# All weight sums in the second FFN, and seven block products in the third

## The chip, the cores and the metric

The kernel runs on one core of one Trainium2 chip. The time is device microseconds of one execution; the kernel before took 922.86 us, the median of three runs (922.39 to 922.95). One execution was profiled.

## The reference, cut to what matters

A trunk of two layers on x of shape (1, 256, 1024), all float32: each layer is half an FFN, a mixer, half an FFN.

```python
h = h + 0.5 * swiglu(rms_norm(h, ffn1_norm[layer]), ffn1_w_gate[layer], ffn1_w_up[layer], ffn1_w_down[layer])
h = h + ab_mixer(...) if layer % 2 == 0 else h + c_mixer(...)
h = h + 0.5 * swiglu(rms_norm(h, ffn2_norm[layer]), ffn2_w_gate[layer], ffn2_w_up[layer], ffn2_w_down[layer])
# swiglu(x, g, u, d) = (silu(x @ g) * (x @ u)) @ d, with D_FF = 2816
```

A last RMS norm follows. So there are four FFNs; the text calls them first (phase 0), second (phase 2), third (phase 3) and last (phase 5). Phases 1 and 4 are the mixers. The second FFN and the third stand next to each other.

## The kernel before, in words

Every product of activations and weights is made of three matmuls (`mm3`, L388 to L390): both operands are split into a high part (`whi`, `xTh`, `hTh`) and the rest (`wlo`, `xTl`, `hTl`), and high x high, rest x high and high x rest are added in one PSUM bank. There are eight banks.

`Stream` brings the weights in one order for the whole kernel, by chunks of up to 128 x 2048. SP issues the loads into three `raw` buffers (L201); ScalarE copies the high part (L249) and VectorE subtracts it (L256), into one of four pairs of buffers (`SPL`). When a chunk has been used up, `free` gives its buffers back, and the next split and the next load are written down there.

An FFN first makes 22 gate and up products (steps n = 0 to 21, one chunk of 48 matmuls each), turns each pair into two tiles of the hidden matrix (`gated`), and then multiplies by the down weights. In the plain form the four blocks of 256 output columns are made one after the other, each from three chunks of 8, 8 and 6 tiles; `pair` (L437, L438, L424, L427) adds a finished block to x and forms `xTh` and `xTl` for the next stage. Behind the second or third gate/up product of a stage `everywhere` makes the norm: VectorE and ScalarE split the sum of squares into `acch` and `accl` (L393), TensorE multiplies both by ones (L481, L482), and a row comes out by which `gated` scales.

In the first FFN alone (`WOVEN = (0,)`) half of the down projection, 512 of 1024 output columns, has another form: a pair of hidden tiles and two tiles of 256 columns make a 2 x 2 product of blocks, which needs seven block products instead of eight. The sums of weight blocks are formed in the `raw` buffer behind the load (L263 to L267), those of hidden blocks in `gated` (L738 to L740). The products (`seven_products`) go to four banks of their own and are woven between the gate/up chunks from the fifth pair on (`LAG = 4`), and between the down chunks. They come out with tokens on the partitions, so `gather_first` adds them up and `turned` transposes them back (eight transposes, L787).

The last FFN uses seven products for nine of its eleven pairs, and needs sums of its weight blocks. These are made earlier: `begin_sums` loads a chunk into `blocks` (L666), three or four subtractions on VectorE form the sums in place (L670 to L676), and `keep` stores them to device memory (L682). `AHEAD` names the steps where a load is issued; the subtractions are written one step later, the stores two. Loads and stores stand in SP's queue behind the weight load last issued before them.

Inside each engine the order is fixed when the program is built: a planner goes through the instructions by their place in the program, with durations that it assumes, and takes the first that it believes to be ready. On the chip each engine then follows that order. `issue_after` binds an instruction behind another on its engine. Each stage opens a pool for its own tiles (`fp` for an FFN, `mp` for a mixer) and closes it at its end; the next stage's pool takes the same memory.

Of the kernel before, what the change touches and what calls it, by code (L numbers as in the profile page):

```python
# [11 lines left out]
F32R = mybir.dt.float32r  # L12
# [8 lines left out]
FT = FF // 128  # L21
# [15 lines left out]
LINE, SHIFT = 64, 16  # L37
EDGE, GAP = 56, 240

RESET, RESHIFT = 3, 52  # L40
# [5 lines left out]
SPARE = 2  # L46
AHEAD = [(phase, n) for phase in (2, 3) for n in (4, 8, 12, 16)] + [(3, 19)]

WOVEN = (0,)
LAG = 4  # L50
MSHIFT, HSHIFT = 16, 56
# [4 lines left out]
def weight_chunks():  # L56
# [10 lines left out]

    def ffn(name, layer, last=False, again=(2, 3), woven=False):
        first = len(chunks)
        wd = (f"{name}_w_down", layer)  # L70

        def seven(pair):
            add(wd, pair * 256, 2, 0, 512, MSHIFT, kind="S")

        for c in range(0, FF, 256):
            if len(chunks) == 0:
                for k in (0, 4):
                    add((f"{name}_w_gate", f"{name}_w_up", layer), k * 128, 4, c, c + 256, SHIFT,
                        (1, 2, 3) if k else (0.5, 1, 1.5, 2, 3))
                continue  # L80
            for m in ("gate", "up"):
                n = len(chunks)
                cuts = (6,) if first == 0 and n in again else ()
                cols((f"{name}_w_{m}", layer), c, 256, cuts,
                     RESET if n - first in again or woven and m == "gate" and c // 256 > LAG else 0)
            if woven and c // 256 >= LAG:
                seven(c // 256 - LAG)
        if last:
            for i in range(FT // 2):
                add(wd, i * 256, 2, 0, D, kind=LAST[i])  # L90
            return
        rest = list(range(FT // 2 - LAG, FT // 2)) if woven else []
        behind = woven
        if woven:
            seven(rest.pop(0))
        for c in range(512 if woven else 0, D, 256):
            for k, n in DOWN:
                add(wd, k * 128, n, c, c + 256, SHIFT, reset=RESET if behind else 0)
                behind = bool(rest)
                if rest:  # L100
                    seven(rest.pop(0))
# [6 lines left out]

    ffn("ffn1", 0, again=(2,), woven=0 in WOVEN)
    wab = ("ab_w_in", 0)  # L110
# [6 lines left out]
    mix(("ab_w_out", 0), MIX1)  # L117
    ffn("ffn2", 0, again=(2,), woven=2 in WOVEN)
    ffn("ffn1", 1, again=(), woven=3 in WOVEN)
    wc = ("c_w_in", 0)  # L120
# [225 lines left out]
def trunk(ctx: ExitStack, tc: tile.TileContext, a, out):  # L346
# [341 lines left out]
    def ffn(phase):  # L688
        nonlocal nxt
        with tc.tile_pool(name="fp", bufs=1) as fp:  # L690
            hT = [fp.tile([128, FT, S], F32R, name=n) for n in ("hTh", "hTl")]
            last = phase == 5
            woven = phase in WOVEN
            if last:
# [21 lines left out]
            ready, ahead = [], []  # L716

            def gated(k, pg, pu):
# [16 lines left out]
                if woven:  # L735
                    f = g.rearrange("p i (t c) -> p (i t) c", t=2)
                    a11, a12 = (hm[:, i, :128] for i in range(2))
                    nc.vector.tensor_sub(f[:, :2], hm[:, 0].rearrange("p (t c) -> p t c", t=2), hm[:, :, 128:])  # L738
                    nc.vector.tensor_sub(f[:, 2], f[:, 1], a11)
                    nc.vector.tensor_add(f[:, 3], a12, f[:, 2])  # L740
                    summed[k // 2] = [fp.tile([128, 4 * 128 + LINE], F32R, name=m, bufs=LAG + 1)[:, HSHIFT : HSHIFT + 512]
                                        .rearrange("p (i c) -> p i c", i=4) for m in ("hSh", "hSl")]
                    split(*summed[k // 2], f)
# [37 lines left out]
            def turned(i, parts):  # L781
# [6 lines left out]
                nxt.pair(i, b, norm["half"], fp)  # L788

            late = {0: 4, 3: 2}.get(phase, 3)  # L790
            if phase in (2, 5):
                split(*parts[:2], nxt.acc[:, 0])
            for n in range(FT):
# [10 lines left out]
                if phase in (2, 5) and n == 1:  # L804

                    nc.tensor.matmul(bank()[:, :1], ones, ones[:, :1], start=True, stop=True)
                if (phase, n) in AHEAD:
                    ahead.append(begin_sums(fp, AHEAD.index((phase, n))))
                if (phase, n - 1) in AHEAD:
                    ahead.append(ahead.pop()())  # L810
                if (phase, n - 2) in AHEAD:
                    ahead.pop()()
                if n == late - 1:
# [15 lines left out]
                elif n > late and m == 1:  # L829
                    gated(k, *ready[-2:])  # L830
                if woven and m == 1 and k // 2 >= LAG:
                    seven_products(k // 2 - LAG)
            if last:
# [6 lines left out]
            nxt = Next(phase + 1)  # L840
            rest = list(range(FT // 2 - LAG, FT // 2)) if woven else []
            if woven:
                seven_products(rest.pop(0))
            for c in range(2 if woven else 0, 4):
                b = bank()
                for k0, n in DOWN:
                    w = st.take()
                    turns = [(j, kk) for kk in range(RESET, n) for j in range(2)]
                    for j, kk in [(j, kk) for j in range(2) for kk in range(RESET)] + turns:
# [3 lines left out]
                            k == j == 0, k == FT - 1 and j == 1)  # L853
                        if woven and c == 3 and k0 == 8 and j and kk in (3, 6):
                            turned(kk // 6, quarters[kk // 6])
                    if k0 + n == FT:
                        nxt.pair(c, b, row, fp)
                    st.free()
                    if rest:
                        seven_products(rest.pop(0))  # L860
                        if not rest:
                            quarters = gather_first()
# [593 lines left out]
```

## Time and profile before

| | |
|---|---|
| median of three runs | 922.86 us |
| the profiled execution | 922.25 us |
| its span, first to last instruction | 920.5 us |
| TensorE busy | 912.8 us |
| VectorE busy | 730.7 us |
| ScalarE busy | 545.3 us |
| DMA traffic over the span | 220 GB/s |

All times in the profile are counted from the start of the span. By the order of TensorE's matmuls the first FFN runs to 182.81, the second from 272.30 to 452.33 and the third from 452.33 to 632.08; the last begins at 739.80.

### The profile page before, as it was taken

Reading aid. Unit: us, or ns where it says so; the run is one execution under the profiler, and the core shown is the slowest. Engines: PE = TensorE matmul, PEld = TensorE weight load, DVE = VectorE, ACT = ScalarE, POOL = GpSimd, SP = SyncE. Lnnn points to the kernel's source line nnn. Section 1 sums busy time; section 2 is a strip of 40 time slices with the busy share of each in tenths; the row PEclk is TensorE's granted clock in tenths of the full one; section 3 lists DMA queues with packets and bytes.
Section 4 is the critical chain, followed back from the end, with each engine's and each line's share of the span. In section 5 each row is a group of like instructions: output and inputs, shape, how many; then the busy total and the mean of one; then the engine's idle time right before and its main releaser. Section 6 shows DMA issues by size and latency. Waiting matters only on the chain.

```text
span 920.5 us, 18362 instructions
## 1 busy us (share of the span) xinstructions
PE 912.8 (99%) x7558; PEld 894.0 (97%) x7558; DVE 730.7 (79%) x1162; ACT 545.3 (59%) x840; POOL 82.1 (9%) x117
## 2 busy tenths in 40 slices
PE   9999999999999999999999999999999999999997
PEld 9999999989999999999999999999999999999886
DVE  7999897997889767655786677666778799878896
ACT  7766555668667544444564454355776777555574
POOL 0000000034310000000000000001565100000002
PEclk9999999999999999999999999999999999999999
DMA  9646555665256777765557877855433566755681
GB/s 331 244 163 239 201 177 204 231 227 183 93 184 229 245 276 266 288 236 214 205 207 271 294 255 295 323 210 199 177 138 138 134 228 223 271 201 194 230 310 54
DMA packets 34707, 202.17 MB, mean 220 GB/s; under 512 B 3984, under 2 KB 6288, under 8 KB 13760
## 3 DMA queue, kind: packets, MB, share of 16 engines
q1 hardware_dynamic: 33120, 197.79, 60.1%
q0 software_dynamic: 496, 1.77, 0.9%
q10 hardware_dynamic: 1008, 1.44, 0.5%
q8 instruction: 59, 0.97, 0.4%
q14 instruction: 24, 0.20, 0.1%
HBM read 188.14 MB, written 12.85 MB: 218 GB/s over the span
## 4 chain that ended last, share of the span: by engine, by line
PE 94%; issue 4%; DVE 1%; POOL 0%; ACT 0%; POOLq 0%; DVEq 0%
PE bank L388 30%; PE bank L389 30%; PE bank L390 30%; PE bank L636 1%; PE bank L1158 1%; DVE wlo L256 1%; PE bank L612 0%; PE bank L639 0%; POOL xTl L902 0%; PE bank L1120 0%; ACT whi L249 0%; PE bank L1122 0%; DVE xTl L427 0%; PE bank L1121 0%; DVE x L438 0%
## 5 line engine op out<-in xcount | busy, mean ns | idle before, releaser
L249 ACT ACTIVATE whi<-raw 128x1024 fp32r<-128x1024 f32 (+5 forms) x369 | 341.6, 970 | 244.0 <-PE bank L389 125.2
L256 DVE TENSOR_TENSOR wlo<-raw,whi 128x1024 fp32r<-128x1024 f32 (+5 forms) x369 | 402.8, 1120 | 56.3 <-ACT whi L249 55.2
L388 PE MATMUL bank<-xTh,whi 128*128 128x256 f32 x1600 | 442.7, 277 | 0.0
L389 PE MATMUL bank<-xTl,whi 128*128 128x256 f32 x1600 | 441.9, 276 | 0.3 <-DVE xTl L427 0.3
L390 PE MATMUL bank<-xTh,wlo 128*128 128x256 f32 x1600 | 441.8, 276 | 0.0
L389 PEld LDWEIGHTS bank<-xTl,whi 128*128 128x128 f32 x1600 | 300.4, 188 | 0.6 <-DVE xTl L427 0.5
L388 PEld LDWEIGHTS bank<-xTh,whi 128*128 128x128 f32 x1600 | 300.4, 188 | 0.0
L390 PEld LDWEIGHTS bank<-xTh,wlo 128*128 128x128 f32 x1600 | 300.4, 188 | 0.0
L388 PE MATMUL bank<-hTh,whi 128*128 128x256 f32 x440 | 121.7, 277 | 0.0
L390 PE MATMUL bank<-hTh,wlo 128*128 128x256 f32 x440 | 121.5, 276 | 0.0
L389 PE MATMUL bank<-hTl,whi 128*128 128x256 f32 x440 | 121.5, 276 | 0.0
L389 PEld LDWEIGHTS bank<-hTl,whi 128*128 128x128 f32 x440 | 82.6, 188 | 0.0
L388 PEld LDWEIGHTS bank<-hTh,whi 128*128 128x128 f32 x440 | 82.6, 188 | 0.0
L390 PEld LDWEIGHTS bank<-hTh,wlo 128*128 128x128 f32 x440 | 82.6, 188 | 0.0
L723 DVE TENSOR_TENSOR hm<-gs,bank 128x512 f32<-128x512 f32 x44 | 29.9, 683 | 34.8 <-PE bank L390 34.6
L1053 POOL MEMSET k<- 64x256 f32 x12 | 3.2, 306 | 563.7 <-ACT whi L249 378.9
L720 DVE TENSOR_TENSOR gs<-bank,row 128x512 f32<-128x512 f32 x44 | 30.1, 685 | 14.0 <-PE bank L390 13.9
L388 PE MATMUL bank<-mixh,whi 128*128 128x256 f32 x128 | 35.7, 279 | 0.0
L1149 POOL TENSOR_SCALAR pr<-pr,rl 128x128 f32<-128x128 f32 (+1 forms) x36 | 33.1, 931 | 28.2 <-DVE rl L1145 19.2
L390 PE MATMUL bank<-mixh,wlo 128*128 128x256 f32 x128 | 35.4, 277 | 0.0
L389 PE MATMUL bank<-mixl,whi 128*128 128x256 f32 x128 | 35.4, 276 | 0.0
L393 ACT ACTIVATE hTh<-hm 128x512 fp32r<-128x512 f32 x44 | 27.2, 619 | 10.4 <-DVE hm L723 9.5
(247 smaller groups left out, 1149.4 us busy)
## 6 DMA issues: line engine op xcount, KB each, us to landing
raw<-in_weights SPq DMA_DIRECT2D x135, 1024.0 KB, 5.0
blocks<-in_weights SPq DMA_DIRECT2D x9, 1024.0 KB, 9.3
blocks<-blocks SPq DMA_DIRECT2D x9, 1024.0 KB, 9.0
raw<-in_weights SPq DMA_DIRECT2D x17, 512.0 KB, 3.5
raw<-in_weights SPq DMA_DIRECT2D x10, 768.0 KB, 6.3
raw<-blocks SPq DMA_DIRECT2D x7, 1024.0 KB, 4.8
raw<-in_weights SPq DMA_DIRECT2D x7, 256.0 KB, 4.7
blocks<-block SPq DMA_DIRECT2D x5, 256.0 KB, 8.7
```

The source lines that it names most:

```text
L249: done = nc.scalar.activation(hi, r, AF.Copy)
L256: self.made[u] = done, nc.vector.tensor_sub(lo, r, hi.bitcast(F32))
L388: nc.tensor.matmul(p, sh, mh, start=start, stop=False)
L389: nc.tensor.matmul(p, sh, ml, start=False, stop=False)
L390: return nc.tensor.matmul(p, sl, mh, start=False, stop=stop)
L393: return nc.scalar.activation(hi, src, AF.Copy), nc.vector.tensor_sub(lo, src, hi.bitcast(F32))
L636: nc.tensor.matmul(o, w[0][i][:, cs], xT[m][:, k], start=k == 0 and m == "h" and j % 2 == 0, stop=False)
L720: nc.vector.tensor_mul(g, both(pg), twice(norm["row"]))
L723: nc.vector.tensor_mul(hm, g, both(pu))
L1053: nc.gpsimd.memset(pair[j][o, 1].bitcast(F32), 0.0)
L1149: share = engine.tensor_scalar(pr[:, cs], pr[:, cs], rl[:, b : b + 1], None, op0=ALU.mult)
L1158: nc.tensor.transpose(tp[:, i * 128 : (i + 1) * 128], pr[:, i * 128 : (i + 1) * 128], ident)
```

## The change

`AHEAD` now names nine steps, all of phase 2, from n = 2 to n = 31: the steps go on over the twelve down chunks (22 to 33), and `sums_at` is called there as well, behind `free`. Phase 3 forms no sums any more.

`WOVEN` and `LAG` become one table, `LAGS = {0: 4, 3: 4}`, so phase 3 is woven as phase 0 is: half of its down projection by seven products, its down weights in eleven chunks of 512 KB and six plain ones. Its summed hidden tiles begin at another offset within their buffers (`at`). In both woven phases the last down chunk (columns 768 on, tiles 16 on) gets the `reset` layout, in which its split is made in three pieces instead of two.

```diff
--- before.py
+++ after.py
@@ -44,10 +44,9 @@
 LAST = "ZZXZXZXXXNN"
 SEVEN = [i for i, c in enumerate(LAST) if c != "N"]
 SPARE = 2
-AHEAD = [(phase, n) for phase in (2, 3) for n in (4, 8, 12, 16)] + [(3, 19)]
-
-WOVEN = (0,)
-LAG = 4
+AHEAD = [(2, n) for n in (2, 6, 10, 13, 17, 21, 24, 28, 31)]
+
+LAGS = {0: 4, 3: 4}
 MSHIFT, HSHIFT = 16, 56
 
 MIX1, MIX2 = (4, 5, 6, 7, 0, 1, 2, 3), (0, 1, 2, 3, 4, 5, 6, 7)
@@ -65,9 +64,11 @@
         for k in range(0, KD, n):
             add(m, k * 128, n, c0, c0 + w, SHIFT if w == 256 else 0, cuts, reset)
 
-    def ffn(name, layer, last=False, again=(2, 3), woven=False):
+    def ffn(name, layer, last=False, again=(2, 3), phase=None):
         first = len(chunks)
         wd = (f"{name}_w_down", layer)
+        lag = LAGS.get(phase, FT)
+        woven = phase in LAGS
 
         def seven(pair):
             add(wd, pair * 256, 2, 0, 512, MSHIFT, kind="S")
@@ -82,20 +83,20 @@
                 n = len(chunks)
                 cuts = (6,) if first == 0 and n in again else ()
                 cols((f"{name}_w_{m}", layer), c, 256, cuts,
-                     RESET if n - first in again or woven and m == "gate" and c // 256 > LAG else 0)
-            if woven and c // 256 >= LAG:
-                seven(c // 256 - LAG)
+                     RESET if n - first in again or woven and m == "gate" and c // 256 > lag else 0)
+            if c // 256 >= lag:
+                seven(c // 256 - lag)
         if last:
             for i in range(FT // 2):
                 add(wd, i * 256, 2, 0, D, kind=LAST[i])
             return
-        rest = list(range(FT // 2 - LAG, FT // 2)) if woven else []
+        rest = list(range(FT // 2 - lag, FT // 2)) if woven else []
         behind = woven
-        if woven:
+        if lag > 2 and woven:
             seven(rest.pop(0))
         for c in range(512 if woven else 0, D, 256):
             for k, n in DOWN:
-                add(wd, k * 128, n, c, c + 256, SHIFT, reset=RESET if behind else 0)
+                add(wd, k * 128, n, c, c + 256, SHIFT, reset=RESET if behind or woven and (c, k) == (768, 16) else 0)
                 behind = bool(rest)
                 if rest:
                     seven(rest.pop(0))
@@ -106,7 +107,7 @@
         for c in (0, 512):
             add(m, order[4] * 128, 4, c, c + 512, SHIFT, summed=summed and c == 0)
 
-    ffn("ffn1", 0, again=(2,), woven=0 in WOVEN)
+    ffn("ffn1", 0, again=(2,), phase=0)
     wab = ("ab_w_in", 0)
     cols(wab, 0, 256)
     cols(wab, 512, 256, reset=RESET)
@@ -115,8 +116,8 @@
     for c, n in ((1536, RESET), (1792, 0), (256, RESET), (768, RESET)):
         cols(wab, c, 256, reset=n)
     mix(("ab_w_out", 0), MIX1)
-    ffn("ffn2", 0, again=(2,), woven=2 in WOVEN)
-    ffn("ffn1", 1, again=(), woven=3 in WOVEN)
+    ffn("ffn2", 0, again=(2,), phase=2)
+    ffn("ffn1", 1, again=(), phase=3)
     wc = ("c_w_in", 0)
     for c in range(4):
         cols(wc, c * 256, 256, reset=RESET if c % 2 else 0)
@@ -690,7 +691,7 @@
         with tc.tile_pool(name="fp", bufs=1) as fp:
             hT = [fp.tile([128, FT, S], F32R, name=n) for n in ("hTh", "hTl")]
             last = phase == 5
-            woven = phase in WOVEN
+            lag, woven = LAGS.get(phase, FT), phase in LAGS
             if last:
                 size = [128, len(SEVEN), 3, 128]
                 early = [fp.tile(size, t, name=n) for t, n in ((F32, "hSh"), (F32R, "hSl"))]
@@ -738,7 +739,8 @@
                     nc.vector.tensor_sub(f[:, :2], hm[:, 0].rearrange("p (t c) -> p t c", t=2), hm[:, :, 128:])
                     nc.vector.tensor_sub(f[:, 2], f[:, 1], a11)
                     nc.vector.tensor_add(f[:, 3], a12, f[:, 2])
-                    summed[k // 2] = [fp.tile([128, 4 * 128 + LINE], F32R, name=m, bufs=LAG + 1)[:, HSHIFT : HSHIFT + 512]
+                    at = 0 if phase else HSHIFT
+                    summed[k // 2] = [fp.tile([128, 4 * 128 + LINE], F32R, name=m, bufs=lag + 1)[:, at : at + 512]
                                         .rearrange("p (i c) -> p i c", i=4) for m in ("hSh", "hSl")]
                     split(*summed[k // 2], f)
                 if seven:
@@ -786,6 +788,15 @@
                         at = j * S + t * 128
                         nc.tensor.transpose(b[:, at : at + 128], parts[t][:, j * 128 : (j + 1) * 128], ident)
                 nxt.pair(i, b, norm["half"], fp)
+
+            def sums_at(n):
+
+                if (phase, n) in AHEAD:
+                    ahead.append(begin_sums(fp, AHEAD.index((phase, n))))
+                if (phase, n - 1) in AHEAD:
+                    ahead.append(ahead.pop()())
+                if (phase, n - 2) in AHEAD:
+                    ahead.pop()()
 
             late = {0: 4, 3: 2}.get(phase, 3)
             if phase in (2, 5):
@@ -804,12 +815,7 @@
                 if phase in (2, 5) and n == 1:
 
                     nc.tensor.matmul(bank()[:, :1], ones, ones[:, :1], start=True, stop=True)
-                if (phase, n) in AHEAD:
-                    ahead.append(begin_sums(fp, AHEAD.index((phase, n))))
-                if (phase, n - 1) in AHEAD:
-                    ahead.append(ahead.pop()())
-                if (phase, n - 2) in AHEAD:
-                    ahead.pop()()
+                sums_at(n)
                 if n == late - 1:
                     if phase not in (2, 5):
                         split(*parts[:2], nxt.acc[:, 0])
@@ -828,8 +834,8 @@
                         gated(i, *ready[i : i + 2])
                 elif n > late and m == 1:
                     gated(k, *ready[-2:])
-                if woven and m == 1 and k // 2 >= LAG:
-                    seven_products(k // 2 - LAG)
+                if m == 1 and k // 2 >= lag:
+                    seven_products(k // 2 - lag)
             if last:
                 wide = [xp.tile([128, KD, S], F32, name=m).rearrange("p k s -> p (k s)") for m in ("xTh", "xTl")]
                 st.spare.append(wide[0])
@@ -838,8 +844,8 @@
                 return
             row = norm["half"]
             nxt = Next(phase + 1)
-            rest = list(range(FT // 2 - LAG, FT // 2)) if woven else []
-            if woven:
+            rest = list(range(FT // 2 - lag, FT // 2)) if woven else []
+            if lag > 2 and woven:
                 seven_products(rest.pop(0))
             for c in range(2 if woven else 0, 4):
                 b = bank()
@@ -851,11 +857,12 @@
                         cs = slice(j * 128, (j + 1) * 128)
                         mm3(b[:, j * S : (j + 1) * S], w[0][kk][:, cs], w[1][kk][:, cs], hT[0][:, k], hT[1][:, k],
                             k == j == 0, k == FT - 1 and j == 1)
-                        if woven and c == 3 and k0 == 8 and j and kk in (3, 6):
+                        if woven and (c, k0) == (3, 8) and j and kk in (3, 6):
                             turned(kk // 6, quarters[kk // 6])
                     if k0 + n == FT:
                         nxt.pair(c, b, row, fp)
                     st.free()
+                    sums_at(FT + 3 * c + k0 // 8)
                     if rest:
                         seven_products(rest.pop(0))
                         if not rest:
```

## Rows read from the trace of the kernel before

**Rows 1.** The page: busy time of TensorE, and its granted clock by slices.
```profile
PE 912.8 (99%) x7558; PEld 894.0 (97%) x7558; DVE 730.7 (79%) x1162; ACT 545.3 (59%) x840; POOL 82.1 (9%) x117
...
PEclk9999999999999999999999999999999999999999
```

**Rows 2.** The page, costliest groups: busy, mean ns | idle before, and what ended it.
```profile
L389 PE MATMUL bank<-xTl,whi 128*128 128x256 f32 x1600 | 441.9, 276 | 0.3 <-DVE xTl L427 0.3
```

**Rows 3.** Windows: length, then PE, PEld, DVE, ACT, POOL busy, clock, DMA.
```profile
572.24:632.08 59.84, 59.84 (x531) 59.84 (x530) 38.38 (x46) 27.53 (x35) 0.00 (x0) 1.00 0.72 262
16.24:190.30 174.06, 173.71 (x1528) 173.52 (x1527) 159.94 (x243) 108.67 (x149) 2.13 (x8) 1.00 0.61 217
463.44:638.88 175.44, 175.44 (x1551) 175.44 (x1550) 122.76 (x148) 87.24 (x110) 2.91 (x9) 1.00 0.72 258
```

**Rows 4.** Timeline of TensorE, first FFN: start, length, instruction; a group of transposes.
```profile
175.09 0.60 PE L787 MATMUL bank<-ident,hm 128*128 128x128 f32 x4
175.45 0.37 PE L388 MATMUL bank<-hTh,whi 128*128 128x256 f32 x1
175.66 0.28 PE L389 MATMUL bank<-hTl,whi 128*128 128x256 f32 x1
```

**Rows 5.** Timeline of TensorE behind the first FFN.
```profile
186.89 0.28 PE L388 MATMUL bank<-xTh,whi 128*128 128x256 f32 x1
187.51 0.39 PE L389 MATMUL bank<-xTl,whi 128*128 128x256 f32 x1 [0.35 <-DVE xTl L427]
```

**Rows 6.** Timeline of VectorE at the same place.
```profile
185.85 1.22 DVE L256 TENSOR_TENSOR wlo<-raw,whi 128x1024 fp32r<-128x1024 f32 x1
```

**Rows 7.** Timeline of VectorE, third FFN: the last two sums.
```profile
560.97 0.69 DVE L670 TENSOR_TENSOR blocks<-blocks 128x512 f32<-128x512 f32 x1 [4.16 <-DMA blocks<-in_weights]
...
565.05 0.68 DVE L676 TENSOR_TENSOR block<-blocks 128x512 f32<-128x512 f32 x1
...
580.74 0.69 DVE L670 TENSOR_TENSOR blocks<-blocks 128x512 f32<-128x512 f32 x1 [4.92 <-DMA blocks<-in_weights]
```

**Rows 8.** Line L1053 from 585 on: durations in ns, first and last start.
```profile
L1053 POOLq EVENT_SEMAPHORE  x3: 42/43/46172, 587.6 to 634.2; - x3
```

**Rows 9.** Timeline of SP: the last store of sums.
```profile
583.39 0.33 SPq L682 DMA_DIRECT2D blocks<-blocks  x1
```

**Rows 10.** Line L682 from 583 to 590: landing of these stores.
```profile
DMA to landing us min/median/max: 4.1/4.2/4.2
```

**Rows 11.** Timeline of ScalarE, start of the third FFN.
```profile
457.81 0.42 ACT L393 ACTIVATE acch<-acc 128x256 fp32r<-128x256 f32 x1 [2.02 <-PE bank L389]
```

**Rows 12.** Timeline of VectorE, start of the third FFN.
```profile
455.00 0.88 DVE L427 SCALAR_TENSOR_TENSOR xTl<-x,gT,xTh 128x256 fp32r<-128x256 f32 x2
...
458.27 0.43 DVE L393 TENSOR_TENSOR accl<-acc,acch 128x256 fp32r<-128x256 f32 x1 [0.55 <-ACT acch L393]
```

**Rows 13.** Timeline of TensorE: the third FFN's first product, and its mean.
```profile
452.33 0.28 PE L388 MATMUL bank<-xTh,whi 128*128 128x256 f32 x1
...
463.21 0.28 PE L481 MATMUL bank<-acch,all_ones 128*128 128x256 f32 x1
```

**Rows 14.** Timeline of SP: weight loads around the end of the second FFN.
```profile
446.38 0.33 SPq L201 DMA_DIRECT2D raw<-in_weights  x1
...
457.45 0.33 SPq L201 DMA_DIRECT2D raw<-in_weights  x1
```

**Rows 15.** Line L666, loads of blocks, whole span: landing.
```profile
DMA to landing us min/median/max: 6.8/9.3/11.6
```

**Rows 16.** Line L682, stores of sums, whole span: landing.
```profile
DMA to landing us min/median/max: 4.1/8.8/10.0
```

**Rows 17.** Timeline of TensorE, first mixer: its mean.
```profile
190.30 0.28 PE L481 MATMUL bank<-mixh,all_ones 128*128 128x256 f32 x1
...
190.77 0.28 PE L482 MATMUL bank<-mixl,all_ones 128*128 128x256 f32 x1
```

**Rows 18.** Line L670: idle time of VectorE before it, and how often.
```profile
  DMA blocks<-in_weights: 26.8, 9
```

## The prediction

> **What bounds the kernel now.** I read the page's busy times first, then the idle time of its costliest groups, then windows of equal work, and last the timelines of single hand-overs. The reader should see that TensorE is busy 912.8 of 920.5 us with its clock at the upper of its two levels, 2.4 GHz, in all slices [rows 1], and that its largest matmul group stood idle for only 0.3 us in all, for an `xTl` of VectorE [rows 2]. So a matmul taken out is time taken out, and any new wait in TensorE's queue is time put in; what other engines do counts only where TensorE waits for it.
>
> The profiled execution took 922.25 us, 1.75 us more than its span of 920.5. The median of the three runs, 922.86, is 0.61 above it; I work in the profiled execution and add 0.61 at the end.
>
> **Term 1: what the third FFN saves on TensorE.** The plain down projection is 528 matmuls of 256 columns in 59.84 us, 0.1133 us each [rows 3]. For each of 11 pairs of hidden tiles, half of the output columns takes 7 products instead of 8, of three matmuls each: 33 matmuls less, -3.74 us. Added are 8 transposes: a group of four holds TensorE from 175.09 to 175.45, and the matmul behind it needs 0.21 instead of 0.11 [rows 4]: 2 x (0.36 + 0.10) = +0.92. The ledger gives -2.8.
>
> The first FFN already has the changed form, so the trace holds a better measure. From the third gate/up product to the twentieth 256-column triple of the next stage it took 174.06 us, the third FFN 175.44 for the same work in the plain form [rows 3]. The first one's window has two matmuls more (the mean's, which in the third stand just before the window), 0.23 us. So the woven form is worth 173.83 - 175.44 = **-1.6 us**. The 1.2 us that the ledger has beyond that are partly a stall at its end: the second matmul of a triple began 0.62 us after the first, for `xTl`, and VectorE had put a 1.22 us weight split, from 185.85, ahead of that `xTl` [rows 5, 6]. I expect the third stage's end to do the same, since the chunks around it have the same shapes. Without that stall (0.51 us) the term would be -2.1; with the ledger whole, -2.8; with twice the stall, -1.1.
>
> VectorE's load in the woven form is no new bound: 159.94 of 174.06 us, and TensorE stood still only at that one place [rows 3, 5]. The third stage now has 122.76 of 175.44 with five sums in it, and loses these.
>
> **Term 2: sums moved into the second FFN.** The second FFN then forms 9 sums, not 4. A sum is three or four VectorE subtractions of 0.69 us; with the splits between them one lasted from 560.97 to 565.73 [rows 7]; back to back three would be 2.1: 2.1 to 4.8 us. Five more are at most 24 us. The third stage, with five sums, left VectorE 52.7 us idle and TensorE never waiting [rows 3], so inside the stage I take 0; the bounds are 0 and 1 us. The transfers (1 MB in, 1 MB or 1.25 MB out) are moved, not added. The reset flag on the last chunk cuts its weight split into three pieces instead of two, on ScalarE and VectorE: 0, bounds -0.5 (it removes the stall above, in either stage) and +0.1. The other offset of the summed tiles: 0.
>
> **Term 3: the end of the second FFN.** The last three sums now fall into the down projection, at n = 24, 28 and 31; the last is stored behind the last chunk. Here I expect the loss.
>
> What the trace shows first: the tiles of a stage's pool are taken over whole. GpSimd's first write into the attention stage's pool waits in steps: one step comes to its turn at 587.6, and the next lasts 46.2 us, to the stage's end [rows 8]. The last stores of sums, the first of them issued at 583.39 [rows 9], landed 4.1 to 4.2 us later [rows 10], the first so at 587.5. That first write is a small `k` tile, which has no use for either. So the first write into the next FFN's pool must wait for the last store too. In the third FFN this is `acch` on ScalarE, at 457.81, then `accl` on VectorE at 458.27 [rows 11, 12], and TensorE multiplies them at 463.21 [rows 13]. Nothing in the kernel before lands late enough to matter there; the changed one's last store does.
>
> When it lands: the second stage's matmuls end at 452.33 [rows 13]; the chunk of n = 31 ends 84 matmuls earlier, at 442.8. Its block load stands in SP's queue behind the weight load now issued at 446.38 [rows 14], so it goes out at 446.8 to 449 (later if sum 28 delays VectorE). Loads of blocks took 6.8 to 11.6 us, median 9.3 [rows 15]; 11.6 was the one just behind the sum before it, three steps earlier, as here. I take landing at 459 (456 to 460.6). The sum ends about 4 us later, at 463. The store is also behind the weight load now issued at 457.45 [rows 14], so it can't leave before 457.8. Stores took 4.1 to 10.0 us, median 8.8 [rows 16]: landing at 471.8 (463.4 to 475.4). `acch`, `accl` and their hand-overs took 0.9 us, so TensorE's mean products can start at about 472.7, 9.5 us after their present place.
>
> How much of the 9.5 is lost depends on where they stand in TensorE's queue, which is fixed when the program is built. The planner moves them: at the first mixer it put three matmuls between the two [rows 17], so it goes by when it believes the operand to be ready. But it believes transfers to be faster than they are: VectorE reached each sum before its blocks had landed and stood there, 26.8 us over nine, 3.0 on average [rows 18], 4.16 and 4.92 in the last two [rows 7]. If it misjudges the last load by 4.9 and the store by nothing, TensorE waits 4.9 us; if it misjudges both by the mean, 6.0. I take **+5.5**; the bounds are 0 (the store's latency is overrated by as much as the load's is underrated) and 9.5 (not moved at all). While it waits, all later products wait; the weight splits on ScalarE behind `acch` wait too, but they run up to four chunks ahead (`SPL`), and TensorE is standing anyway. The norm row comes late by as much, and the gated products with it; eight banks cover that.
>
> Two rules of the Trainium skill bear on this. Its page "TensorE: Matmul & The Clock Gate" (section "The mechanism") says that matmuls start and end strictly in program order; by that rule no later product can pass the waiting mean product, which speaks against the change, and the trace agrees: behind the late `xTl` the whole queue stood 0.62 us [rows 5]. Its page "DMA: Bandwidth & Descriptors" (section "Anatomy of one DMA", on the other descriptor path) gives about 2.0 us plus bytes over 436 GB/s; as an estimate a 1 MB store would take 4.4 us, land at 467.4, and cap the loss at about 5.2, net +3.6. The trace agrees for the one store at 583.39 (4.1) and not for the median of 8.8 [rows 9, 10, 16]; I keep the rows.
>
> **Sum.** -1.6 + 0 + 5.5 = +3.9: 922.25 + 3.9 + 0.61 = **926.8 us**.
>
> **Rivals.**
> 1. *The first FFN is repeated and the store costs nothing*: -1.6, **921.3**. For it: the planner may place the mean products late enough, since nothing needs the norm row for several products. Against it: nine of nine waits for blocks fell on the side where the transfer was later than planned [rows 18].
> 2. *As 1, and the reset piece takes the stall away at the end of one or both woven stages*: -2.1 to -2.8, 920.1 to 920.7, say **920.4**. Against it: that chunk's split lies some 10 us ahead of its use and isn't what VectorE was late with [rows 6].
> 3. *The last sum is placed ahead of the last pair's `xTl` on VectorE.* `xTl` ran from 455.00 to 455.9 [rows 12], and TensorE needs it 36 matmuls after 452.33, at 456.5. If VectorE waits for the blocks first (459), then forms them (4) and then the pair (2), TensorE loses 8.4 us there, and nothing more at the mean products: +6.8, **929.7**. It decides from the order of the block subtraction and `xTl` in VectorE's queue. Against it: with the planner's usual 7 to 10 us from issue the blocks look ready only after 453.8, about when the pair is done.
> 4. *Three sums spaced by three steps overload the transfers and weights come late in the second stage*: +1 to +3 on top of rival 1, **923.3**. Against it: a 92% busy VectorE starved nothing in the first FFN [rows 3].
>
> **How the numbers follow.** Below 921.0 is faster by over 0.2% (1.85 us, about what a measurement of this kernel tells from no change), above 924.7 slower. Forecast 0.52: slower if the wait is over 3.4 us, 0.43, else same 0.09. Rival 1, 0.26, lies 0.3 above the bound: same 0.13, faster 0.13. Rival 2, 0.08, faster. Rival 3, 0.09: slower 0.07, same 0.02. Rival 4, 0.05: same 0.03, slower 0.02. Faster 0.21, same 0.27, slower 0.52. The forecast's own range is 922 to 930.8 (waits of 0.7 to 9.5); with rivals 1 and most of 2 the range is 920.3 to 930.5.
>
> **What would show it.** Term 1: the third stage's down projection with 33 matmuls less and 8 transposes, its window some 1.6 us shorter apart from new waits, a stall of about 0.5 us on `xTl` behind it. Term 3: one idle gap of TensorE within the first 25 us of the third FFN, ended by `acch` or `accl`; `acch` starting within 0.2 us of the landing of the last store of sums, near 472 instead of 457.81; VectorE idle some 4 us before the last block subtraction. The prediction is wrong if `acch` starts before that store has landed, if the mean products lie so late in TensorE's queue that there is no gap, or if the gap stands at `xTl` instead.

## The result, and the profile after

The changed kernel takes 936.14 us (median of 4 runs, 934.70 to 937.24), the kernel before 922.64 beside it: ratio 1.0145, 95% interval 1.0128 to 1.0163, so 13.5 us slower. 926.8 was predicted, with a range up to 930.5. The sign was right and part of the cause; the size was not.

The page, busy times and the granted clock by slices, against [rows 1]: TensorE has 25 matmul records fewer, and the clock is no longer full everywhere.

```profile
span 934.2 us, 18472 instructions
PE 915.8 (98%) x7533; PEld 896.2 (96%) x7533; DVE 774.3 (83%) x1268; ACT 561.4 (60%) x874; POOL 81.8 (9%) x117
PEclk9999999999999999999889999999999999999999
```

What TensorE waited for (us in total, times, longest). Before, it had one wait of 0.35 us inside the work [rows 5]; now there are two long ones. The 0.8 us on its sequencer (PEq) stands in both kernels.

```profile
PE bank L482 <- ACT acch L394: 5.8, 1, 5.8
PE bank L389 <- ACT xTh L425: 5.0, 1, 5.0
PE bank L613 <- PEq L1450: 0.8, 1, 0.8
PE bank L390 <- DVE xTl L428: 0.3, 1, 0.3
```

Both lie at the start of the third FFN. Timeline of TensorE there (start, length, instruction, idle time before and what ended it), against [rows 13]:

```profile
461.51 0.58 PE L389 MATMUL bank<-xTh,whi 128*128 128x256 f32 x1 [4.99 <-ACT xTh L425]
...
462.63 0.41 PE L389 MATMUL bank<-xTh,whi 128*128 128x256 f32 x1
462.84 0.41 PE L390 MATMUL bank<-xTl,whi 128*128 128x256 f32 x1
...
476.97 0.58 PE L482 MATMUL bank<-acch,all_ones 128*128 128x256 f32 x1 [5.83 <-ACT acch L394]
```

Windows over the same stretch (length; PE, PEld, DVE, ACT, POOL busy; clock; DMA share; GB/s):

```profile
456.00:462.00 6.00, 1.01 (x6) 0.61 (x4) 3.94 (x6) 2.94 (x5) 0.00 (x0) 0.81 0.98 366
462.00:472.00 10.00, 9.13 (x60) 8.90 (x59) 7.23 (x10) 3.28 (x4) 0.00 (x0) 0.77 0.97 409
472.00:478.00 6.00, 1.03 (x4) 1.03 (x5) 2.79 (x3) 2.59 (x4) 0.00 (x0) 0.62 1.01 352
478.00:482.00 4.00, 4.00 (x28) 4.00 (x27) 3.37 (x5) 0.63 (x2) 0.00 (x0) 0.72 0.55 231
482.00:486.00 4.00, 4.00 (x37) 4.00 (x37) 2.22 (x5) 3.85 (x5) 0.00 (x0) 1.00 0.00 0
```

So there are three losses. The gaps are 4.99 + 5.83 = 10.8 us. Behind each gap the matmuls follow one another at 0.21 us instead of 0.113 (462.63, 462.84): the clock is at its lower level, 1.2 GHz (0.50 granted from 462 to 466). From 452.28 to 522.40 TensorE ran 482 matmuls of 256 columns, 54.6 us at 0.1133, in 70.1 us: 15.5 lost, 10.8 of it in gaps and 4.7 to the clock and to refilling the pipeline. The profiled execution as a whole is 13.7 us longer (span 934.2 against 920.5), since the woven third FFN gives 1.8 back.

**The second gap is the predicted one.** SP's stores of the last sum, then `acch` on ScalarE:

```profile
470.24 0.33 SPq L683 DMA_DIRECT2D blocks<-blocks  x1
470.84 0.33 SPq L683 DMA_DIRECT2D blocks<-block  x1
```

```profile
DMA to landing us min/median/max: 5.6/5.6/5.6
```

```profile
476.50 0.42 ACT L394 ACTIVATE acch<-acc 128x256 fp32r<-128x256 f32 x1 [3.39 <-DMA blocks<-block]
```

The later store landed at 470.84 + 5.6 = 476.4, and `acch` began at 476.50. Before, it began at 457.81 [rows 11].

**The first gap was not predicted.** Its chain, read backwards, on ScalarE, SP and VectorE:

```profile
459.06 2.00 ACT L250 ACTIVATE whi<-raw 128x1024 fp32r<-128x1024 f32 x2 [8.69 <-DMA raw<-in_weights]
460.97 0.89 ACT L425 ACTIVATE xTh<-x,gT 128x256 fp32r<-128x256 f32 x2
```

```profile
436.78 0.43 SPq L667 DMA_DIRECT2D blocks<-in_weights  x1
438.13 14.30 SPq L202 DMA_DIRECT2D raw<-in_weights  x2
452.48 0.42 SPq L683 DMA_DIRECT2D blocks<-blocks  x1
```

```profile
445.87 0.69 DVE L671 TENSOR_TENSOR blocks<-blocks 128x512 f32<-128x512 f32 x1 [6.44 <-DMA blocks<-in_weights]
446.48 1.22 DVE L257 TENSOR_TENSOR wlo<-raw,whi 128x1024 fp32r<-128x1024 f32 x1
...
450.82 1.22 DVE L257 TENSOR_TENSOR wlo<-raw,whi 128x1024 fp32r<-128x1024 f32 x1
...
457.55 0.69 DVE L439 TENSOR_TENSOR x<-part,x 128x512 f32<-128x512 f32 x1
```

`xTh` needs only the `x` that VectorE formed by 458.2. But it stands in ScalarE's queue behind a weight split, and that split waits for a weight that landed at 459.0. SP issued this weight (the second of the two in the row at 438.13) only at 452.10, because the raw buffer came free with the end of VectorE's split from 450.82, at 452.04. That split stood behind the sum of chunk 28, for whose blocks VectorE had waited 6.44 us. Of these waits there are seven, 33.2 us in all; before, nine with 26.8 [rows 18].

### The profile page after: what moved, and what is told of

Read it like the earlier page. It is cut to its first block, busy times and chain, and to the rows that moved or that the text cites. A ratio compares the mean times of both kernels' runs of the same rounds, so it can differ in the third digit from the quotient of the medians.

```text
span 934.2 us, 18472 instructions
## 1 busy us (share of the span) xinstructions
PE 915.8 (98%) x7533; PEld 896.2 (96%) x7533; DVE 774.3 (83%) x1268; ACT 561.4 (60%) x874; POOL 81.8 (9%) x117
## 4 chain that ended last, share of the span: by engine, by line
PE 93%; DVE 2%; DMA 2%; issue 1%; ACT 1%; POOLq 0%; POOL 0%; SPq 0%; DVEq 0%; ACTq 0%
PE bank L389 30%; PE bank L390 30%; PE bank L391 29%; DVE wlo L257 1%; DMA blocks<-in_weights 1%; PE bank L637 1%; PE bank L1165 1%; DMA raw<-in_weights 1%; DMA blocks<-block 1%; ACT whi L250 0%; PE bank L613 0%; PE bank L640 0%; DVE xTl L428 0%; PE bank L1127 0%; PE bank L1129 0%
## 5 line engine op out<-in xcount | busy, mean ns | idle before, releaser
L389 PE MATMUL bank<-hTh,whi 128*128 128x256 f32 x352 | 97.7, 278 | 0.0
L391 PE MATMUL bank<-hTh,wlo 128*128 128x256 f32 x352 | 97.3, 276 | 0.0
L390 PE MATMUL bank<-hTl,whi 128*128 128x256 f32 x352 | 97.3, 276 | 0.0
L391 PEld LDWEIGHTS bank<-hTh,wlo 128*128 128x128 f32 x352 | 66.1, 188 | 0.0
L389 PEld LDWEIGHTS bank<-hTh,whi 128*128 128x128 f32 x352 | 66.1, 188 | 0.0
L390 PEld LDWEIGHTS bank<-hTl,whi 128*128 128x128 f32 x352 | 66.1, 188 | 0.0
L394 ACT ACTIVATE hSh<-gs 128x512 fp32r<-128x512 f32 (+1 forms) x31 | 18.6, 601 | 33.5 <-DVE gs L741 17.9
L389 PE MATMUL bank<-whi,hTh 128*128 128x256 f32 (+1 forms) x114 | 36.1, 316 | 0.0
L390 PE MATMUL bank<-wlo,hTh 128*128 128x256 f32 (+1 forms) x114 | 36.0, 316 | 0.0
L391 PE MATMUL bank<-whi,hTl 128*128 128x256 f32 (+1 forms) x114 | 36.0, 316 | 0.0
```

The lines of the kernel that those rows point to most:

```text
L389: nc.tensor.matmul(p, sh, mh, start=start, stop=False)
L390: nc.tensor.matmul(p, sh, ml, start=False, stop=False)
L391: return nc.tensor.matmul(p, sl, mh, start=False, stop=stop)
L394: return nc.scalar.activation(hi, src, AF.Copy), nc.vector.tensor_sub(lo, src, hi.bitcast(F32))
```

## Experiments

### No sums in the last chunks: e1_early, e9_early_plain, e7_early_noreset

e1_early:
```diff
-AHEAD = [(2, n) for n in (2, 6, 10, 13, 17, 21, 24, 28, 31)]
+AHEAD = [(2, n) for n in range(1, 26, 3)]
```


> The nine sums begin at n = 1, 4, ... 25 instead of 2 to 31, so the last store is written 6 chunks before the end of the second FFN. Theory (the loss is made at the end of the second FFN alone, by sums whose load, subtractions and store run into the next stage): no gap of TensorE at the start of the third FFN, the woven third FFN gives its 1.6 us, about 921 us, 0.998 of before. Rival (nine sums are too many for the second FFN wherever they stand; steps of three overload the transfers and VectorE): gaps inside the second FFN, over 925 us.

Measured: 920.81 us, ratio 0.9982 (0.9972 to 0.9991). The gaps and the lower clock are gone; the window at the same place:

```profile
458.00:464.00 6.00, 6.00 (x55) 6.00 (x54) 3.20 (x5) 2.32 (x3) 0.00 (x0) 1.00 0.58 193
```

All nine sums are still in the second FFN, so their number costs nothing: what costs is where the last ones stand. VectorE's idle time before the sums falls from 33.2 to 1.5 us. This version is better than both kernels.

e9_early_plain is e1_early with a plain third FFN:
```diff
-LAGS = {0: 4, 3: 4}
+LAGS = {0: 4}
```


> The nine sums as in e1_early (at every third chunk, the last at 25), and the third FFN left plain: its down projection is not woven and makes no block products. Theory (the seven block products are worth what the prediction's first term says, 1.6 us, and the early sums cost nothing): e1_early plus 1.6, 922.1 to 922.8 us, the third FFN's stage as long as before. Rival A (the products give nothing, e1_early's gain is that of moving the sums out of the third FFN): as e1_early, 920.5 to 921.1. Rival B (the products give more and the sums cost something): above 923.

Measured: 922.57 us, ratio 1.0002 (0.9993 to 1.0011): as the kernel before. So the moved sums by themselves are worth 0, and weaving the third FFN is worth 0.9982 - 1.0002 = -0.0020, 1.8 us. The traces agree: from the third FFN's first matmul to the kernel's last, 459.67 us in e1_early and 461.41 in e9_early_plain.

e7_early_noreset is e1_early without the added reset:
```diff
-                add(wd, k * 128, n, c, c + 256, SHIFT, reset=RESET if behind or woven and (c, k) == (768, 16) else 0)
+                add(wd, k * 128, n, c, c + 256, SHIFT, reset=RESET if behind else 0)
```


> e1_early without the one reset that the change adds at row 16 of the last column group of both woven down projections. Theory (the reset has taken away the first FFN's end stall of 0.35 us, which stands at 0.03 in the trace of e1_early, and about as much at the third FFN's end): 0.3 to 0.7 us above e1_early, 921.1 to 921.6, with the stall of 0.3 or more back near 187.5. Rival (the reset moves nothing): 920.5 to 921.1, no stall there.

Measured: 920.99 us, ratio 0.9982 (0.9973 to 0.9991), the same as e1_early within what can be told. The trace shows why: the reset moves the stall from one woven stage to the other. First e1_early, then e7_early_noreset:

```profile
635.05 0.39 PE L390 MATMUL bank<-xTl,whi 128*128 128x256 f32 x1 [0.30 <-DVE xTl L428]
```

```profile
188.04 0.38 PE L390 MATMUL bank<-xTl,whi 128*128 128x256 f32 x1 [0.35 <-DVE xTl L428]
```

### The two gaps one at a time: e2_own, e3_order, e4_both

e2_own gives the third FFN's norm tiles memory that the blocks never used:
```diff
-            else:
+            elif phase != 3:
                 parts = [fp.tile([128, S], F32R, name=n) for n in ("acch", "accl")]
...
-                    if phase not in (2, 5):
+                    if phase == 3:
+                        q = wk.tile([128, 2, S], F32R, name="sq", bufs=1)
+                        split(q[:, 0], q[:, 1], nxt.acc[:, 0])
+                        v = wk.tile([128, 2, S], F32, name="acc", bufs=1)
+                        m = wk.tile([128, NT, 128], F32, name="wide", bufs=1)
+                        parts = [q[:, 0], q[:, 1], m.rearrange("p t c -> p (t c)"), v[:, 0], v[:, 1]]
+                    elif phase not in (2, 5):
...
```


> The changed kernel, but in the third FFN the operands of the mean and the three tiles behind them lie in buffers of the long-lived pool that are free by then (those of sq, acc and wide), so their first write does not follow the closing of the second FFN's pool. Theory (acch waits for the last store of sums because the pool is taken over whole): acch starts near 464 to 466 instead of 476.5, the gap of 5.83 us at L482 and the half-clock stretch behind it go, the gap of 5.0 us at xTh stays: 927 to 929 us. Rival (the mean's products wait for something else that is late, such as the squares or VectorE): the gap stays, 935 to 937 us.

Measured: 927.43 us, ratio 1.0050 (1.0035 to 1.0066), 8.7 us less than the changed kernel's median. The tile that stands for `acch` (named `sq` here) no longer waits for a transfer, although the last sums' stores go out only from 467.57 on:

```profile
461.75 0.42 ACT L394 ACTIVATE sq<-acc 128x256 fp32r<-128x256 f32 x1 [2.02 <-DVE acc L462]
```

This shows that `acch` waited for the store only because its pool lies on the memory of the blocks. The first gap, expected to stay at 5.0 us, was 1.96 in the profiled execution; the part on the first gap comes back to this.

e3_order keeps the weight split out of the way: what `st.free()` issues behind the last chunk follows the last pair's `xTh`:
```diff
-                    if k0 + n == FT:
-                        nxt.pair(c, b, row, fp)
-                    st.free()
+                    with ExitStack() as behind:
+                        if k0 + n == FT:
+                            high, _ = nxt.pair(c, b, row, fp)
+                            if phase == 2 and c == 3:
+                                behind.enter_context(tc.issue_after(high.ins))
+                        st.free()
```


> The changed kernel, but on ScalarE the weight split written behind the second FFN's last chunk is queued behind the last pair's xTh instead of ahead of it. Theory (two waits in a row, of which the second ends at a fixed time, the landing of the last store): the gap at xTh shrinks from 5.0 to about 2 us, and the one at L482 grows by as much, 935 to 937 us, no change beyond the clock. Rival (the two waits add up): 3 us and some clock less, 931 to 933 us.

Measured: 934.77 us, ratio 1.0125 (1.0110 to 1.0140), between the two bands and nearer the theory's; by its time alone the 1.4 us to the changed kernel can hardly be told from no change. In the trace the first gap is gone, so ScalarE's order made it; but the second grew from 5.83 to 9.38 us, because `acch` still waits for the store:

```profile
473.37 0.58 PE L482 MATMUL bank<-acch,all_ones 128*128 128x256 f32 x1 [9.38 <-ACT acch L394]
```

```profile
472.90 0.42 ACT L394 ACTIVATE acch<-acc 128x256 fp32r<-128x256 f32 x1 [3.93 <-DMA blocks<-block]
```

e4_both makes both edits.

> Both edits of the two runs before together. Theory (two separate waits, the second hiding what the first one costs): gap at L482 gone and gap at xTh down to about 2 us, so more than the sum of the two single effects, 923 to 925 us. Rival (the effects add): the change of the one plus the change of the other.

Measured: 924.54 us, ratio 1.0022 (1.0011 to 1.0032), 11.6 us less than the changed kernel, where the two edits alone gave 8.7 and 1.4. The 1.5 us between the sums lie within what these intervals tell. That the gaps do not add is shown by the trace of e3_order: of the 4.99 us taken away at `xTh`, 3.55 came back at the mean. While both are there, the second hides most of the first. What is left is 1.37 us at `xTh`, now for VectorE's `x` itself, and the clock behind it:

```profile
458.43 0.38 PE L389 MATMUL bank<-xTh,whi 128*128 128x256 f32 x1 [1.37 <-ACT xTh L425]
```

```profile
458.00:464.00 6.00, 5.44 (x30) 5.24 (x31) 4.43 (x7) 3.50 (x6) 0.00 (x0) 0.72 1.01 423
```

### What makes the first gap: e5_unwoven, e10_last28, e11_no31, e13_no28, e12_lead

e5_unwoven is the changed kernel with `LAGS = {0: 4}`.

> The changed kernel's nine sums (the last at chunk 31), the third FFN plain. Theory (the loss lies wholly at the end of the second FFN and has nothing to do with the third FFN's form): the same two gaps of about 5 and 6 us, and 1.6 us more than the changed kernel, 936.5 to 939.5. Rival (the woven third FFN's own order of chunks, its first weight loads among them, makes part of the wait): the first gap under 3 us, 927 to 934.

Measured: 936.85 us, ratio 1.0174 (1.0138 to 1.0211), gaps of 4.24 and 5.3 us at the same two places (in a profiled execution of 944.81 us, on which the last part has more). The loss doesn't come from the woven third FFN.

e10_last28:
```diff
-AHEAD = [(2, n) for n in (2, 6, 10, 13, 17, 21, 24, 28, 31)]
+AHEAD = [(2, n) for n in (1, 4, 8, 11, 15, 18, 22, 25, 28)]
```


> Nine sums in the second FFN, the last at chunk 28 (1, 4, 8, 11, 15, 18, 22, 25, 28), the rest as in the changed kernel. Theory (two causes apart: acch waits for the store of the sum at 31, and the last pair's high part comes late because VectorE stood 6.4 us for the load of the sum at 28): the gap of 5.83 us before the mean products is gone, one of 4 to 5.5 us before the first product with the last pair's high part stays, with 1 to 3 us of lower clock: 925.5 to 929.5. Rival (both waits come from the sum at 31, whose load takes its place in SP's queue ahead of weights): neither gap, 920.5 to 922.5.

Measured: 921.28 us, ratio 0.9995 (0.9985 to 1.0004). My theory fell: with VectorE standing 4.91 us for the blocks of chunk 28, TensorE waited only 0.5 us for `xTh` (profiled execution 925.21 us). Since the other sums had moved too, I ran the two kernels that differ from the changed one in the last sums and the first ones only:

```diff
-AHEAD = [(2, n) for n in (2, 6, 10, 13, 17, 21, 24, 28, 31)]
+AHEAD = [(2, n) for n in (0, 3, 6, 10, 13, 17, 21, 24, 28)]   # e11_no31
+AHEAD = [(2, n) for n in (0, 3, 6, 10, 13, 17, 21, 24, 31)]   # e13_no28
```


> The changed kernel with the sum at chunk 31 taken away and one put at the front instead: 0, 3, 6, then 10, 13, 17, 21, 24 and 28 as in the changed kernel. e10_last28 had neither gap, but its sums from 1 to 25 stood at other chunks too. Theory (what the sums at 10 to 28 cost VectorE is enough for the first gap): a gap of 3 to 5 us before the first product with the last pair's high part, none at the mean products, 925 to 929. Rival (the sum at 31 makes both): no gap above 1 us, 920.5 to 922.5.

> The counterpart of e11_no31: the sum at chunk 28 taken away and the one at 31 kept (0, 3, 6, 10, 13, 17, 21, 24, 31). e11_no31 had neither gap, so the sum at 28 alone makes none. Theory (the first gap needs the sums at 28 and 31 together, VectorE being behind from the one when the other's traffic comes; the second needs the one at 31 alone, and ends a few hundredths of a microsecond behind the last store's landing): no gap above 1.5 us at the last pair's high part, one of 6 to 11 us at the mean products, 929 to 936. Rival (the sum at 31 makes both alone): a gap of 3 us and more at the last pair's high part and one of about 6 at the mean products, 935 to 938.

Measured: e11_no31 921.85 us, ratio 1.0001 (0.9985 to 1.0017), ten runs from 920.89 to 928.39; e13_no28 931.69 us, ratio 1.0101 (1.0084 to 1.0117). In e11_no31 neither gap is there:

```profile
457.08 0.38 PE L389 MATMUL bank<-xTh,whi 128*128 128x256 f32 x1 [0.19 <-ACT xTh L425]
```

In e13_no28 there is the second alone; its load, its stores, and what follows them:

```profile
447.20 0.42 SPq L667 DMA_DIRECT2D blocks<-in_weights  x1
452.31 8.70 SPq L202 DMA_DIRECT2D raw<-in_weights  x2
461.06 1.22 SPq L683 DMA_DIRECT2D blocks<-blocks  x1
462.33 0.43 SPq L683 DMA_DIRECT2D blocks<-block  x1
```

```profile
470.96 0.42 ACT L394 ACTIVATE acch<-acc 128x256 fp32r<-128x256 f32 x1 [4.30 <-DMA blocks<-block]
```

```profile
471.43 0.58 PE L482 MATMUL bank<-acch,all_ones 128*128 128x256 f32 x1 [6.74 <-ACT acch L394]
```

So e13_no28 bears its theory out: the sum at 31 makes the second gap by itself, and the first gap is long only in kernels that have both. (e13_no28 waits 0.5 us for `xTl` besides.) The four make a table by the last sums:

| last sums | kernel | ratio to before | gap at `xTh` | gap at the mean |
|---|---|---|---|---|
| 22, 25 | e1_early | 0.9982 | 0 | 0 |
| 24, 28 | e11_no31 | 1.0001 | 0.19 | 0 |
| 24, 31 | e13_no28 | 1.0101 | 0 | 6.74 |
| 28, 31 | changed | 1.0145 | 4.99 | 5.83 |

The traces of e11_no31 and the changed kernel are nearly alike until the load of chunk 28 goes out (at 436.16 and 436.78), and its sum begins 2.9 us earlier in e11_no31:

```profile
439.22 1.22 DVE L257 TENSOR_TENSOR wlo<-raw,whi 128x1024 fp32r<-128x1024 f32 x1
443.00 0.69 DVE L671 TENSOR_TENSOR blocks<-blocks 128x512 f32<-128x512 f32 x1 [2.56 <-DMA blocks<-in_weights]
```

Its blocks landed after 6.8 us instead of 9.0, and one 1.22 us split lies ahead of it that in the changed kernel lies behind (446.48 above). So the buffer came free, and the late weight was issued, at 448.1 instead of 452.1. That is 4.0 of the 4.8 us between the two gaps.

The same chain can be followed in other traces, by the end of this split on VectorE, the issue of the late weight on SP, and the gap:

| kernel | split ends | weight issued | gap at `xTh` |
|---|---|---|---|
| changed | 452.04 | 452.10 | 4.99 |
| e5_unwoven | 452.19 | 452.26 | 4.24 |
| e2_own | 449.44 | 449.51 | 1.96 |
| e11_no31 | 448.03 | 448.09 | 0.19 |
| e10_last28 | 443.35 | 443.41 | 0.5 |

In e2_own the order is that of the changed kernel; the blocks landed after 7.9 us instead of 9.0, and the gap was 3 us shorter. In e10_last28 the split stands ahead of the sum of chunk 28, so VectorE's wait for blocks did not hold up this buffer, and what TensorE waited for there was the last `x` itself. VectorE and SP in e10_last28:

```profile
442.13 1.22 DVE L257 TENSOR_TENSOR wlo<-raw,whi 128x1024 fp32r<-128x1024 f32 x1
...
448.59 0.69 DVE L671 TENSOR_TENSOR blocks<-blocks 128x512 f32<-128x512 f32 x1 [4.91 <-DMA blocks<-in_weights]
```

```profile
438.38 5.36 SPq L202 DMA_DIRECT2D raw<-in_weights  x2
```

So the theory lacked the order: in these traces VectorE's wait cost TensorE time only where the split that frees the buffer stood behind it. Why the sum at 31, whose load goes out later, leads to this order and to slower loads wasn't settled.

e12_lead issues every load of blocks one chunk earlier:
```diff
-                if (phase, n) in AHEAD:
-                    ahead.append(begin_sums(fp, AHEAD.index((phase, n))))
+                if (phase, n + 1) in AHEAD:
+                    ahead.append(begin_sums(fp, AHEAD.index((phase, n + 1))))
                 if (phase, n - 1) in AHEAD:
-                    ahead.append(ahead.pop()())
+                    formed.append(ahead.pop(0)())
                 if (phase, n - 2) in AHEAD:
-                    ahead.pop()()
+                    formed.pop(0)()
```


> The changed kernel with each of the nine loads issued one chunk earlier, the sums and the stores at the same chunks as in the changed kernel. Theory (the first gap comes from VectorE standing for loads, 33.2 us before seven sums; the second from the last store's landing): VectorE's idle time before the sums falls under 8 us, the first gap is under 1 us, the second one to 5 us, 922 to 929. Rival (the transfers are the bound, an earlier load only holds up the weights behind it in SP's queue): VectorE's idle moves to the weights, gaps of 8 us and more in all, 932 or more.

Measured: 936.68 us, ratio 1.0142 (1.0124 to 1.0161), gaps of 6.4 and 5.3 us; the rival was right in the time and wrong in its reason. VectorE's idle time stayed at its sums, and rose:

```profile
DVE blocks L671 <- DMA blocks<-in_weights: 38.4, 8, 8.0
```

The last two loads did go out earlier, at 433.15 and 449.84 instead of 436.78 and 455.05, but VectorE still came to eight of the nine sums before their blocks had landed, and the loads' median time to landing rose from 9.1 to 10.0 us. Why the earlier issue gained nothing isn't shown. `xTh`, first in line on ScalarE this time, waited for an `x` that VectorE formed only after the last sum's blocks. That is the prediction's rival 3, with `xTh` in the place of `xTl` and the gap at the mean beside it.

## Why the prediction was wrong

**Term 1 was right**: -1.6 predicted, -1.8 measured (e1_early against e9_early_plain). The stall at the third stage's end came, with 0.30 us instead of 0.5; the reset flag, taken at 0, moves it only.

**Term 2 was right for sums that end early**: 0 predicted, ratio 1.0002 measured by e9_early_plain. With sums at 28 and 31 it was not, as follows.

**Term 3 saw one wait where there were two, and priced it at full clock**: +5.5 predicted. Against e1_early, which has no long gap and the same woven stage, the changed kernel loses 0.0163, 15 us. In the profiles it is 14.8 us: 4.99 at `xTh`, 5.83 at the mean, and 4.0 for the lower clock and the refill (0.7 less than counted above, since e1_early comes to the third FFN 0.74 us later). So the one wait that was forecast measured 5.83, and 9.0 of the 9.5 us by which 5.5 falls short of 15 are the other two.

*The step that failed first* is that everything ahead of the mean products was put at nothing. Term 2 takes 0 inside the stage, and term 3 lets the weight splits "run up to four chunks ahead (`SPL`)". What held the weights here was not the `SPL` pairs but a `raw` buffer: VectorE, standing for the blocks of chunk 28, gave it back only at 452.04, the weight went out at 452.10, and ScalarE had that weight's split ahead of `xTh`: 4.99 us. It takes both late sums: the changed kernel loses 0.0044, 4 us, more than e13_no28. The prediction had this delay only in passing ("later if sum 28 delays VectorE"). Rival 4 named late weights, and took them for a matter of the second stage and of 1 to 3 us; its argument against (a busy VectorE starved nothing in the first FFN) was about VectorE's load, whereas here VectorE stood idle at the head of its queue.

*The clock was a term left out.* In the profiles, e13_no28 is 9.4 us longer than e1_early (928.8 against 919.4), 7.2 of it gaps, so about 2.2 went to the lower level and the refill; in the changed kernel 4.0. I priced the wait as if TensorE went on at full speed behind it.

*"The planner moves them" failed too.* The mean products lie 96 matmuls behind the stage's first in the kernel before, the changed one and every run here. The evidence for moving was three matmuls at the first mixer [rows 17]; that shows a planner that can reorder, not by how much it would here. What it costs alone is seen in e13_no28: a wait of 6.74 us, not 5.5, and not the 9.5 that the prediction had for "not moved at all" either. TensorE came to the mean products at 471.43 - 6.74 = 464.69 instead of 463.21, `acch` began at 470.96 instead of 471.8, and the hand-over took 0.5 instead of 0.9. That 5.5 lies so near the changed kernel's 5.83 is luck: there the first gap had delayed both TensorE and the last load.

*The steps to the landing* held in part. In e13_no28 the load went out at 447.20 (446.8 to 449 predicted) and the stores took 8.6 to 9.2 us (8.8). But the blocks landed at 454.7, not 459, and the sum was done at 458.7, not 463; the stores then stood behind a weight load and left at 461.06 and 462.33. That `acch` came within 1 us of the forecast is two errors against each other.

**The signs named.** `acch` within 0.2 us of the landing: yes, 0.1 or less. The gap near 472: it ended at 476.97, since the load of chunk 31 went out at 455.05, behind the first gap's late weights. VectorE idle some 4 us before the last sum: no, it came to that sum late, and had stood before seven of the others. The third stage 1.6 us shorter, apart from new waits: yes, by 1.8 in e1_early. "The prediction is wrong if ... the gap stands at `xTl` instead": the first gap stands at `xTh`, beside the one at `acch`.

## What to carry to other kernels

When a pool's memory is taken over by the next stage, the last transfer out of the old tiles bounds the first write of the new stage, whatever that write is: give the early tiles of the new stage memory of their own, or end the side work several chunks before the stage does (here, with the last store six chunks before the end, 15 us). A wait at the head of one engine's queue should be followed through the buffers that the work behind it frees, to the loads that need them. When a planner's order decides what a late operand costs, price the case in which it does not move.

## What the runs showed of the hardware

Behind the gaps of 4.99 and 5.83 us TensorE came back at the lower clock level, for 5.0 and 3.2 us: 0.62 to 0.81 granted in the windows from 456 to 482, with matmuls 0.21 us apart against 0.113 at full clock (485.00 and 485.11 in the same trace). The length of the one gap ahead doesn't decide alone: 1.37 us in e4_both was followed by a window at 0.72, while in e2_own, with 1.96 us, the window is at full clock:

```profile
458.00:464.00 6.00, 5.00 (x41) 4.81 (x42) 4.78 (x8) 3.98 (x7) 0.00 (x0) 1.00 1.01 425
```

There is a second, smaller slowing that the granted clock doesn't show. Windows of the kernel before and of e10_last28:

```profile
470.00:510.00 40.00, 40.00 (x355) 40.00 (x354) 29.84 (x35) 22.18 (x28) 0.00 (x0) 1.00 0.71 255
470.00:510.00 40.00, 40.00 (x342) 40.00 (x341) 35.19 (x54) 22.81 (x30) 0.00 (x0) 1.00 0.47 159
```

TensorE is busy throughout at a granted clock of 1.00 in both, but in e10_last28 the matmuls follow one another at 0.1178 us instead of 0.1133. This pace began behind a wait at the start of the third FFN and held for tens of microseconds in four profiled executions: by my sum over the matmuls it makes about 2.5 us in e10_last28, 2.3 in e2_own, 1.7 in e12_lead and 6.9 in e5_unwoven, so these spans are longer by more than gaps and clock. The changed kernel and e13_no28, with longer gaps, don't have it. What sets it isn't shown.
